# One hand-written order on TensorE, cut down: in latent attention only exact scores and value products stay chained

## The chip, the cores and the metric

The kernel runs on one core of one Trainium2 chip. The metric is the device time of one execution in microseconds (us), as the median of several runs. Engines are named PE (TensorE, the matrix unit), DVE (VectorE), ACT (ScalarE), POOL (GpSimd) and SP (SyncE, which issues the DMAs here).

## What is computed

The reference is a two-layer network over 1024 latent tokens with 256 context tokens in front of them, width 1024, in float32. Each layer modulates its input, projects it, runs three kinds of token mixing side by side (gated linear attention, retention, and softmax attention from a latent), projects back, and ends in a gated convolutional feed-forward part. The change touches only the softmax attention:

```python
def _mla_attend(qn, qr, kn, kr, v):
    s = (jnp.einsum('bqhd,bkhd->bhqk', qn, kn)
         + jnp.einsum('bqhr,bkr->bhqk', qr, kr)).astype(jnp.float32) * MLA_SCALE
    p = jax.nn.softmax(s, axis=-1).astype(v.dtype)
    return jnp.einsum('bhqk,bkhe->bqhe', p, v)
```

There are 8 heads, with 64 plain and 32 rotated features for queries and keys and 64 for values; `qn`, `kn` and `v` are products of two normalised latents (256 and 128 wide). Latent tokens attend to all 1280 tokens, context tokens to the 256 context tokens, and the second layer needs no context output.

## The kernel before

All activations lie with features on partitions and tokens along the free axis. A layer runs in stages: projection of two halves of 640 tokens, then the token mixing, then output projection, layer norm and feed-forward. The token mixing of a layer is one stretch in which two generators are woven together (`weave`, 1.5 steps of `lin` for one of `mla`): `lin` makes the linear attention and retention (lines up to L812, many small operations on every engine), `mla` the softmax attention. Generators fix the order in which instructions are written; the scheduler of the language then places each engine's instructions by priority and by its own estimate of when they are ready. Each engine then executes its own list in order.

`mla` (from L822) makes for each head h:

- production, `prod_kq(h)`: the rotated query rows are copied by DMA (L901), then nine matmuls (seven in the second layer) give plain keys and queries (L912, L915) in PSUM banks 0 to 2; ACT copies them out rounded (L921) and DVE writes the rest that rounding lost (L922). `prod_qr` (L879, L886) makes the rotated queries of four heads, `prod_v` (L867) the values of two.
- `maxima(h)`: rough scores, one matmul each (L934), in three banks taken in turn ("pre", banks 0 to 2), each reduced to a row maximum on DVE (L935): 26 of them in the first layer and 24 in the second. When all are there, one small reduction (L937), a transpose of the maxima on PE (L941), an ACT copy (L942), and two DMAs, out to memory (L943) and back as row 96 of the query tile (L944), so that the exact scores come out with the maximum taken off.
- exact scores, `products` (L951): three matmuls into one of three other banks ("sc", banks 3 to 5), then an exponential on ACT (L1042) into a tile P. Seven such tiles exist.
- `values` (L957): P times V into bank 6. A value or sum product is float32 and shows as two matmuls in the trace. DVE adds P tiles up (L1053), so that only two are left for the sums.
- `quotient`: the sums of P by a product with ones (L969, in a bank of "pre"), reciprocal by ACT and DVE (L974 to L977), product (L981), store (L983).

Head h's scores and values are written together with the production and the maxima of head h+1 (`beside()`, two steps of them for each group of three score matmuls). Two sets of key tiles and two of query tiles exist, so the tiles of head h+2 are those of head h, and their copies (L901) wait for the last score of head h.

What sets the order of these matmuls on PE is `pin`: it adds to each matmul a dependency without a semaphore on the matmul pinned before it, so the scheduler must keep them in the written order:

```python
        def pin(x):
            if prev[0] is not None:
                self.tc.add_manual_dep(x.ins, prev[0].ins.name, ...)
            prev[0] = x
```

Before, every matmul of `mla` is pinned. Those of `lin` are not: they are placed between.

Of the kernel before, what the change touches and what calls it, by code (L numbers as in the profile page):

```python
# [74 lines left out]
class Net:  # L75
# [750 lines left out]
    def mla(self, l, S):  # L826
# [4 lines left out]
        nc, a = self.nc, self.a  # L831
        ww = []
        for k, n in (("uqn", 512), ("uqr", 256), ("ukv", 512)):
            t = self.ws([128, 2, n])
            nc.sync.dma_start(t[:], a[k][l])
            ww.append(t)
        wn, wr, wk = ww
# [8 lines left out]
        def bank(what):  # L846

            turn[what] = (turn[what] + 1) % 3
            return self.ps[:, turn[what] + (3 if what == "sc" else 0), :]

        def three():
            return self.ps[:, base[0]:base[0] + 3, :].rearrange("p a b -> p (a b)")
# [3 lines left out]
        def pin(x):  # L856

            if prev[0] is not None:
                self.tc.add_manual_dep(x.ins, prev[0].ins.name, mybir.DependencyInfo(mybir.DependencyClass.NoSync, mybir.DependencyReason.DATA),
                                       reason="in order")  # L860
            prev[0] = x

        def prod_v(p):
            V[p] = [self.hid([128, 5, 128]) for _ in range(2)]
            ps = three()
            for t_ in range(10):
                pin(nc.tensor.matmul(ps[:, 128 * t_:128 * t_ + 128], S.ckv[:, 128 * t_:128 * t_ + 128], wk[:, 1, 128 * p:128 * p + 128],  # L867
                                 start=True, stop=True))
            for i in range(2):
                nc.scalar.copy(V[p][i][:].rearrange("p a b -> p (a b)"), ps[:, 640 * i:640 * i + 640])  # L870
            yield

        def prod_qr(x):
            QR[x] = [self.yk(F32R), self.yk(F32R)]
            ps, raw = three(), QR[x][1]
            chunks = [(o, min(512, T - o), ps[:, o - lo:min(512 + o, T) - lo]) for o in range(lo, T, 512)]
            for o, n, t in chunks:
                for kc in range(2):
                    pin(nc.tensor.matmul(t, wr[:, kc, 128 * x:128 * x + 128], S.cq[kc][:, o:o + n], start=(kc == 0), stop=(kc == 1)))  # L879
                nc.scalar.copy(raw[:, o:o + n].bitcast(F32), t)  # L880
            for o, n, t in chunks:
                r = raw[:, o:o + n].bitcast(F32)
                t2, co, si = self.tt([128, 512]), self.tt([128, 512]), self.tt([128, 512])
                nc.sync.dma_start(co[:, 0:n], a["mcos"][:, o:o + n])
                nc.sync.dma_start(si[:, 0:n], a["msin"][:, o:o + n])
                pin(nc.tensor.matmul(t, self.permm[:], r, start=True, stop=True))  # L886
                nc.vector.tensor_tensor(t2[:, 0:n], t, si[:, 0:n], op=ALU.mult)
                nc.vector.tensor_tensor(r, r, co[:, 0:n], op=ALU.mult)
                nc.vector.tensor_tensor(r, r, t2[:, 0:n], op=ALU.add)
                self.split(QR[x][0][:, o:o + n], raw[:, o:o + n], r)  # L890
                del t2, co, si
            yield

        def prod_kq(h):
            K = Kt[h % 2]
            Q[h] = [self.hs([128, T]) for _ in range(2)]
            rr = slice(32 * (h % 4), 32 * (h % 4) + 32)
            for x in range(2):
                for o in range(lo, T, 512):
                    c = slice(o, min(o + 512, T))  # L900
                    nc.sync.dma_start(Q[h][x][64:96, c].bitcast(F32), QR[h // 4][x][rr, c].bitcast(F32))  # L901
            if h < 2:
                for b in range(2):
                    cs = slice(640 * b, 640 * b + 640)
                    self.split(K[0][64:96, cs], K[1][64:96, cs], S.kr[b][64:96, :])
            if h == 1:
                S.kr.clear()
            yield
            ps = three()
            for o, t, kb in ((CTX, ps[:, 0:512], 1), (CTX + 512, ps[:, 512:1024], 1), (0, ps[:, 1024:1280], 0)):  # L910
                n = 512 if kb else CTX
                pin(nc.tensor.matmul(t[0:64, 0:n], wk[:, 0, 64 * h:64 * h + 64], S.ckv[:, o:o + n], start=True, stop=True, skip_group_check=True))  # L912
                if o >= lo:
                    for kc in range(2):
                        pin(nc.tensor.matmul(t[64:128, 0:n], wn[:, kc, 64 * h:64 * h + 64], S.cq[kc][:, o:o + n],  # L915
                                         start=(kc == 0), stop=(kc == 1), skip_group_check=True))
            for o, t, n in ((CTX, ps[:, 0:1024], 1024), (0, ps[:, 1024:1280], CTX)):
                for X, r in ((K, 0), (Q[h], 64)):
                    if r and o < lo:
                        continue  # L920
                    nc.scalar.copy(X[0][0:64, o:o + n], t[r:r + 64])  # L921
                    nc.vector.tensor_tensor(X[1][0:64, o:o + n], t[r:r + 64], X[0][0:64, o:o + n].bitcast(F32), op=ALU.subtract)  # L922
            yield

        def maxima(h):

            k0, q0 = Kt[h % 2][0], Q[h][0]
            mx, part = self.sm([128, 10]), self.sm([128, 8, 3])
            for qi in range(lo // 128, 10):
                nk = CTX if qi < 2 else T  # L930
                for j, o in enumerate(range(0, nk, 512)):
                    n = min(512, nk - o)
                    t = bank("pre")[:, 0:n]
                    pin(nc.tensor.matmul(t, q0[0:96, 128 * qi:128 * qi + 128], k0[0:96, o:o + n], start=True, stop=True))  # L934
                    nc.vector.tensor_reduce(mx[:, qi:qi + 1] if qi < 2 else part[:, qi - 2, j:j + 1], t, axis=AX.X, op=ALU.max)  # L935
                    yield
            nc.vector.tensor_reduce(mx[:, 2:10], part[:], axis=AX.X, op=ALU.max)  # L937
            yield
            n = 10 - lo // 128
            t, r = bank("pre"), self.dgt()  # L940
            pin(nc.tensor.matmul(t[0:n, 0:128], mx[:, 10 - n:10], self.ident[:], start=True, stop=True))  # L941
            nc.scalar.activation(r[0:n, :], t[0:n, 0:128], AF.Copy, scale=-1.0)  # L942
            nc.sync.dma_start(S.mx[h, 10 - n:10, :], r[0:n, :].bitcast(F32))  # L943
            nc.sync.dma_start(q0[96:97, lo:T].bitcast(F32), S.mx[h:h + 1].rearrange("h a b -> h (a b)")[:, lo:T])  # L944
            yield
# [14 lines left out]
        def quotient(h, c0, n, sums):  # L960

            r = 64 * (h % 2)
            o, ov, rb, u = ob[h // 2], self.tt([128, n]), self.tt([128, n]), self.tt([128, n])
            nc.scalar.copy(ov[:], self.pb("av")[:, 0:n])
            yield
            t = bank("pre")[:, 0:n]
            for x, P in enumerate(sums):
                for i in range(2):
                    pin(nc.tensor.matmul(t[64 * i:64 * i + 64, :], self.ones[:, 0:64], P[:, i], start=(x == 0), stop=(x == len(sums) - 1),  # L969
                                         skip_group_check=True))  # L970
            sums.clear()
            del P

            nc.scalar.activation(rb[:], t, AF.Ln)  # L974
            nc.scalar.activation(rb[:], rb[:], AF.Exp, scale=-1.0)
            nc.vector.tensor_tensor(u[:], t, rb[:], op=ALU.mult)
            nc.vector.scalar_tensor_tensor(rb[:], u[:], -2.0, rb[:], op0=ALU.add, op1=ALU.mult)  # L977
            yield
            for i in range(2):
                hs = slice(64 * i, 64 * i + 64)  # L980
                nc.vector.scalar_tensor_tensor(o[r:r + 64, c0 + n * i:c0 + n * i + n], ov[hs, :], -1.0, rb[hs, :], op0=ALU.mult, op1=ALU.mult)  # L981
            if h % 2:
                nc.sync.dma_start(S.m[:, 4 + h // 2, c0:c0 + 2 * n], o[:, c0:c0 + 2 * n])  # L983
            yield
# [10 lines left out]
        for _ in chain(prod_v(0), prod_qr(0), prod_kq(0)):  # L995
            yield
# [4 lines left out]
        for h in range(8):  # L1001
# [3 lines left out]
            if h < 7:  # L1005
                if (h + 1) % 4 == 0:
                    g.append(prod_qr((h + 1) // 4))
                g += [prod_kq(h + 1), maxima(h + 1)]
                if (h + 1) % 2 == 0:
                    g.append(prod_v((h + 1) // 2))  # L1010
# [6 lines left out]
            if l == 0:  # L1017
                P = [self.w2([128, 2, 128], F32) for _ in range(2)]
                for kt in range(2):
                    t = bank("sc")[:, 0:256]  # L1020
# [14 lines left out]
            for kt in range(0, 12, 2):  # L1035
                if kt < 10:
                    for k in (kt, kt + 1):
                        held[k] = self.w2([128, 2, 512], F32)
                        for i in range(2):
                            t = bank("sc")  # L1040
# [6 lines left out]
                if kt >= 2:  # L1047
                    for k in (kt - 2, kt - 1):
                        P = held[k]
# [441 lines left out]
```

## Time and profile before

| | us |
|---|---|
| median of three runs (lowest to highest) | 3589.85 (3583.57 to 3593.07) |
| the profiled execution's own time | 3592.44 |
| its span, first to last instruction | 3590.7 |
| PE busy in the span | 3398.0 (95%) |
| DVE busy | 2288.0 (64%) |
| ACT busy | 1433.9 (40%) |
| POOL busy | 329.3 (9%) |
| mean granted clock of PE, share of full | 0.959 |

Busy times are unions of an engine's intervals; matmuls overlap in the record, so a price of one is better read from start to start. "Idle before" counts what an engine waited before a group, with what released it. The granted clock is the share of full speed that PE had. The rows that are used below come from the page, from its tables of busy time by stretch, from its lists of waits, and from its timelines.

### The profile page before, as it was taken

The page shows a single profiled execution, that of the slowest core. Times are in us where ns is not written, and L with a number is a line of the kernel's source. Part 1 is how long each engine was busy: PE and PEld are TensorE (multiplying, and loading weights), DVE is VectorE, ACT ScalarE, POOL GpSimd, SP SyncE. Part 2 cuts the span into 40 slices and gives each one's busy share as a digit, 9 for nine tenths or more (in the row PEclk, how much of TensorE's full clock was granted, in tenths as well). Part 3 has the DMA queues.
Part 4 walks back from the last instruction along what each step waited for, and adds up shares of the span by engine and source line. Part 5 has one row for each costly group of instructions (what it writes and reads, how often), then busy time and mean ns, then how long its engine had stood idle before and what let it go on. Part 6 is the DMA issues. An engine that isn't in the chain of part 4 may idle for free. (4 is left out here: it accounts for less than half of the span.)

```text
span 3590.7 us, 50954 instructions
## 1 busy us (share of the span) xinstructions
PE 3398.0 (95%) x20366; PEld 2762.3 (77%) x20366; DVE 2288.0 (64%) x3467; ACT 1433.9 (40%) x2403; POOL 329.3 (9%) x487
## 2 busy tenths in 40 slices
PE   8997988889999999999999999788899999999998
PEld 6995544445999999999999897444456788888897
DVE  4336686876785444675557645777676775587555
ACT  3333343434363332353333443334334544345433
POOL 0001122211010000000000000222120000000001
PEclk9998897989999999999999998889899999999999
DMA  8554011123223333422223434011014222223221
GB/s 293 198 176 120 28 35 42 34 83 135 71 71 118 118 118 128 149 101 77 77 73 117 170 124 135 19 30 47 30 54 155 94 94 94 97 92 118 94 95 48
DMA packets 174702, 354.64 MB, mean 99 GB/s; under 512 B 15648, under 2 KB 92912, under 8 KB 174464
## 3 DMA queue, kind: packets, MB, share of 16 engines
q1 hardware_dynamic: 174464, 351.38, 29.4%
q8 instruction: 160, 2.62, 0.3%
q14 instruction: 78, 0.64, 0.1%
HBM read 310.09 MB, written 36.51 MB: 97 GB/s over the span
## 5 line engine op out<-in xcount | busy, mean ns | idle before, releaser
L323 PE MATMUL ps<-h,w 128*128 128x320 f32 (+5 forms) x9600 | 1676.0, 335 | 21.4 <-ACT h L212 12.6
L323 PEld LDWEIGHTS ps<-h,w 128*128 128x128 f32 x9600 | 1535.5, 190 | 158.3 <-ACT h L212 14.8
L213 DVE TENSOR_TENSOR w<-ws,w 128x1024 fp32r<-128x1024 f32 x360 | 440.3, 1223 | 589.2 <-PE ps L323 299.6
L1202 PE MATMUL ps<-hid,w 128*128 128x256 f32 (+4 forms) x3696 | 576.5, 316 | 1.5 <-ACT hid L212 1.5
L1202 PEld LDWEIGHTS ps<-hid,w 128*128 128x128 f32 x3696 | 538.8, 189 | 36.1 <-issue 7.6
L212 ACT CAST w<-ws 128x1024 fp32r<-128x1024 f32 x360 | 379.1, 1054 | 410.6 <-PE ps L1202 291.1
L951 PE MATMUL ps<-h,h 96*128 96x512 f32 (+3 forms) x1008 | 317.3, 436 | 3.8 <-DMA h<-mx 2.3
L1042 ACT ACTIVATE w<-ps 128x512 f32<-128x512 f32 x320 | 189.9, 596 | 284.6 <-PE ps L951 280.9
L951 PEld LDWEIGHTS ps<-h,h 96*128 96x128 f32 (+1 forms) x1008 | 189.5, 205 | 107.9 <-issue 70.2
L1169 DVE SCALAR_TENSOR_TENSOR t<-u,vec,t 128x642 f32<-128x642 f32 (+3 forms) x176 | 144.6, 822 | 183.2 <-ACT t L1168 183.1
L935 DVE TENSOR_REDUCE sm<-ps 128x1 f32<-128x512 f32 (+1 forms) x400 | 222.9, 588 | 52.3 <-PE ps L934 50.2
L1163 ACT COPY u<-ps 128x512 f32<-128x512 f32 (+4 forms) x264 | 118.2, 483 | 316.5 <-PE ps L323 316.5
L1207 DVE SCALAR_TENSOR_TENSOR y<-ps,mod,y 128x320 f32<-128x320 f32 (+5 forms) x376 | 197.2, 558 | 67.8 <-PE ps L1202 67.3
L934 PE MATMUL ps<-h,h 96*128 96x512 f32 (+1 forms) x400 | 153.3, 442 | 50.5 <-DVE sm L935 26.5
L1053 DVE TENSOR_TENSOR w<-w,w 128x1024 f32<-128x1024 f32 x128 | 176.8, 1382 | 24.2 <-PE ps L957 18.4
L957 PE MATMUL ps<-w,hid 128*64 128x512 f32 (+1 forms) x704 | 183.7, 618 | 0.0
L716 POOL TENSOR_TENSOR hid<-hid,hid 128x512 f32<-128x512 f32 x108 | 160.6, 1505 | 137.9 <-ACT hid L696 75.3
L1159 POOL MEMSET u<- 128x1 f32 (+1 forms) x264 | 21.2, 102 | 1647.1 <-DVE t L1170 1451.7
L934 PEld LDWEIGHTS ps<-h,h 96*128 96x128 f32 x400 | 84.2, 217 | 99.9 <-DVE sm L935 48.9
L1168 ACT ACTIVATE t<-u,vec 128x642 f32<-128x642 f32 (+3 forms) x176 | 153.7, 873 | 0.4
L1170 DVE SCALAR_TENSOR_TENSOR t<-u,vec,t 128x642 f32<-128x642 f32 (+3 forms) x176 | 144.4, 820 | 11.4
L212 ACT CAST hid<-t 128x642 fp32r<-128x642 f32 (+3 forms) x88 | 59.5, 676 | 204.7 <-DVE t L1174 204.7
(197 smaller groups left out, 2972.4 us busy)
## 6 DMA issues: line engine op xcount, KB each, us to landing
ws<-in_up_dram SPq DMA_DIRECT2D x176, 512.0 KB
ws<-in_down_dram SPq DMA_DIRECT2D x88, 512.0 KB
ws<-in_ada_dram SPq DMA_DIRECT2D x80, 512.0 KB
ws<-in_w_in_dram SPq DMA_DIRECT2D x48, 512.0 KB
ws<-in_w_out_dram SPq DMA_DIRECT2D x32, 512.0 KB
y<-in_ada_dram SPq DMA_DIRECT2D x16, 512.0 KB
ws<-in_w_v_dram SPq DMA_DIRECT2D x16, 512.0 KB
hid<-in_xT_dram SPq DMA_DIRECT2D x16, 320.0 KB
```

What stands on the lines that cost most here:

```text
L212: self.nc.scalar.copy(hi, src)
L213: self.nc.vector.tensor_tensor(lo, src, hi.bitcast(F32), op=ALU.subtract)
L323: nc.tensor.matmul(ps[:, i, 0:n], w_[:, k, :], h[k][:, part, o:o + n], start=(k == 0 and q == 0), stop=(k == 7 and q == 2))
L716: nc.gpsimd.tensor_tensor(X[n][:], blk(E[n][:, 0, cs[i]]), qx[:], op=ALU.mult)
L934: pin(nc.tensor.matmul(t, q0[0:96, 128 * qi:128 * qi + 128], k0[0:96, o:o + n], start=True, stop=True))
L935: nc.vector.tensor_reduce(mx[:, qi:qi + 1] if qi < 2 else part[:, qi - 2, j:j + 1], t, axis=AX.X, op=ALU.max)
L951: pin(nc.tensor.matmul(t, Kt[h % 2][ka][0:rows, 128 * kt:128 * kt + 128], Q[h][qa][0:rows, c0:c0 + n], start=(x == 0), stop=(x == 2)))
L957: pin(nc.tensor.matmul(op[64 * i:64 * i + 64, 0:n], V[h // 2][kt // 5][:, kt % 5, r:r + 64], P[:, i], start=(kt == 0), stop=last, skip_gro ...
L1042: nc.scalar.activation(held[k][:, i], t, AF.Exp, scale=MSCALE)
L1053: nc.vector.tensor_tensor(A[:], A[:], P[:], op=ALU.add)
L1202: nc.tensor.matmul(pb[i][:, 0:n], w[w_][:, x, ms], p.hh[f0 + x][hp][:, o - 1:o - 1 + n], start=(x == 0 and q == 0), stop=(x == gn - 1 and ...
L1207: nc.vector.scalar_tensor_tensor(t, pb[i][:, o:o + n], self.md(l, 5, m, who), t, op0=ALU.mult, op1=ALU.add)
```

## The change

The pin is taken off six kinds of matmul: the value production (L867), the rotated queries (L879, L886), the key and query production (L912, L915), the rough scores (L934), the transpose of the maxima (L941) and the sums' products (L969). The exact scores (L951) and the value products (L957) stay pinned, now only behind each other. No instruction is added or removed: PE executes the same matmuls in another order, within the two token-mixing stretches alone, and the lists of DVE, ACT and SP are ordered anew there too. POOL's list is the same.

```diff
-                pin(nc.tensor.matmul(ps[:, 128 * t_:128 * t_ + 128], S.ckv[:, 128 * t_:128 * t_ + 128], wk[:, 1, 128 * p:128 * p + 128],
-                                 start=True, stop=True))
+                nc.tensor.matmul(ps[:, 128 * t_:128 * t_ + 128], S.ckv[:, 128 * t_:128 * t_ + 128], wk[:, 1, 128 * p:128 * p + 128],
+                                 start=True, stop=True)
...
-                    pin(nc.tensor.matmul(t, q0[0:96, 128 * qi:128 * qi + 128], k0[0:96, o:o + n], start=True, stop=True))
+                    nc.tensor.matmul(t, q0[0:96, 128 * qi:128 * qi + 128], k0[0:96, o:o + n], start=True, stop=True)
```

(and the same at L879, L886, L912, L915, L941 and L969).

Place 1 is PE's list at the production for head 6 in the first layer: the last matmul of production (L915), the matmuls of `lin` (L727), the sums of head 4 (L969), head 5's value products for the context (L957), its exact scores for the latent tokens (L951, from `h_4997` and `h_4998`, head 5's queries), and the first rough scores of head 6 (L934). Before:

```order
L915 MATMUL ps<-y_373,ws_2543 64x256
L727 MATMUL ps<-hid_5366,hid_5335 32x256 x4
L727 MATMUL ps<-hid_5378,hid_5342 32x128 x4
L727 MATMUL ps<-hid_5433,hid_5353 32x128 x4
L969 MATMUL ps<-w_5055,ones 64x512 x2
L969 MATMUL ps<-w_5234,ones 64x512 x2
L957 MATMUL ps<-w_5390,hid_4893 64x128 x2
L957 MATMUL ps<-w_5391,hid_4893 64x128 x2
L951 MATMUL ps<-h_4997,h_2551 128x512
L951 MATMUL ps<-h_4998,h_2551 128x512
L951 MATMUL ps<-h_4997,h_2552 128x512
L934 MATMUL ps<-h_2549,h_5400 128x256 x2
```

After:

```order
L915 MATMUL ps<-y_373,ws_2543 64x256
L951 MATMUL ps<-h_4997,h_2551 128x256
...
L957 MATMUL ps<-w_5390,hid_4893 64x128 x2
L957 MATMUL ps<-w_5391,hid_4893 64x128 x2
L951 MATMUL ps<-h_4997,h_2551 128x512
L951 MATMUL ps<-h_4998,h_2551 128x512
L951 MATMUL ps<-h_4997,h_2552 128x512
...
L727 MATMUL ps<-hid_5366,hid_5335 32x256 x4
...
L969 MATMUL ps<-w_5055,ones 64x512 x2
L969 MATMUL ps<-w_5234,ones 64x512 x2
L934 MATMUL ps<-h_2549,h_5400 128x256 x2
```

The exact scores of the context (six) and eight groups of the latent scores, 24 matmuls, now stand between the production and the sums of head 4; before there were only the twelve matmuls of `lin`.

Place 2 is PE's list at the transpose of head 7's maxima (L941) in the first layer. `h_5400` and `h_5401` are the queries of head 6, `h_5832` those of head 7; L934 is head 7's rough scores, L957 head 6's values. Before:

```order
L934 MATMUL ps<-h_2551,h_5832 128x512
L934 MATMUL ps<-h_2551,h_5832 128x256
...
L727 MATMUL ps<-hid_6103,hid_6068 32x128 x4
L941 MATMUL ps<-ident,sm_5892 10x128
L951 MATMUL ps<-h_5400,h_2549 128x512
L951 MATMUL ps<-h_5401,h_2549 128x512
L951 MATMUL ps<-h_5400,h_2550 128x512
...
L957 MATMUL ps<-w_6154,hid_5706 64x512 x2
L957 MATMUL ps<-w_6169,hid_5706 64x512 x2
L951 MATMUL ps<-h_5832,h_2551 128x256
```

After:

```order
L957 MATMUL ps<-w_6169,hid_5706 64x512
L934 MATMUL ps<-h_2551,h_5832 128x512
L957 MATMUL ps<-w_6169,hid_5706 64x512
L934 MATMUL ps<-h_2551,h_5832 128x512
L934 MATMUL ps<-h_2551,h_5832 128x256
L727 MATMUL ps<-hid_6090,hid_6037 32x256 x4
...
L969 MATMUL ps<-w_5887,ones 64x512
L941 MATMUL ps<-ident,sm_5892 10x128
L969 MATMUL ps<-w_5887,ones 64x512
L727 MATMUL ps<-hid_6152,hid_6037 32x256 x4
...
L735 MATMUL ps<-hm,hid_6116 128x4 x2
L951 MATMUL ps<-h_5832,h_2551 128x256
```

The transpose moved from a place with 18 scores and 12 value products of head 6 behind it to one behind the last of them; between it and head 7's first score stand one product of the sums and matmuls of `lin`.

Place 3 is SP's list around the two DMAs of head 6's maxima (L943, L944); the L901 are the copies for head 7's queries. Before:

```order
L797 DMA u_5868<-v_88 128x2x256
L943 DMA mx_92<-dg_5692 10x128
L944 DMA h_5400<-mx_92 1x1280
L655 DMA hid_5781<-gate_86 128x2x256
L901 DMA h_5832<-y_4538 32x512 x2
L901 DMA h_5832<-y_4538 32x256
L901 DMA h_5833<-y_4539 32x512 x2
L901 DMA h_5833<-y_4539 32x256
```

After:

```order
L797 DMA u_5868<-v_88 128x2x256
L901 DMA h_5832<-y_4538 32x512 x2
L901 DMA h_5832<-y_4538 32x256
L901 DMA h_5833<-y_4539 32x512 x2
L943 DMA mx_92<-dg_5692 10x128
L901 DMA h_5833<-y_4539 32x256
L944 DMA h_5400<-mx_92 1x1280
```

Five of head 7's six copies moved ahead of the store of the maxima, and one lies between it and the load.

## Rows read from the trace of the kernel before

**Rows 1.** The page's first line: the span of the profiled execution.

```profile
span 3590.7 us, 50954 instructions
```

**Rows 2.** Busy time by stretch, both attention stretches: stretch, length, engines, PEclk, DMA share, GB/s.

```profile
354.50:867.00 512.50, 452.14 (x2308) 248.30 (x2301) 389.29 (x619) 204.91 (x430) 126.14 (x96) 0.90 0.15 47
2253.50:2717.00 463.50, 408.59 (x1919) 221.19 (x1913) 347.91 (x514) 177.61 (x349) 103.96 (x79) 0.89 0.14 44
```

**Rows 3.** PE's waits, first layer's stretch: waiter, releaser, total us, times, longest us.

```profile
PE ps L969 <- DVE h L922: 16.4, 4, 8.6
PE ps L934 <- DVE sm L935: 11.0, 11, 1.9
PE ps L941 <- DVE sm L937: 9.2, 5, 3.1
...
PE ps L912 <- DVE t L976: 4.7, 1, 4.7
```

**Rows 4.** PE's waits, second layer's stretch.

```profile
PE ps L934 <- DVE h L922: 10.5, 6, 2.9
PE ps L941 <- DVE sm L937: 9.2, 5, 2.9
PE ps L934 <- ACT h L921: 8.1, 3, 4.7
PE ps L934 <- DVE sm L935: 6.7, 5, 4.1
```

**Rows 5.** PE timeline: start us, length us, group, count, [idle before <-releaser].

```profile
689.15 1.08 PE L727 MATMUL ps<-hid,hid 128*32 128x256 f32 x24
698.86 3.68 PE L969 MATMUL ps<-w,ones 128*64 128x512 f32 x8 [8.63 <-DVE h L922]
```

**Rows 6.** VectorE in the same moment, same columns.

```profile
694.17 1.21 DVE L1053 TENSOR_TENSOR w<-w,w 128x1024 f32<-128x1024 f32 x1
695.30 1.54 DVE L922 TENSOR_TENSOR h<-ps,h 64x1024 fp32r<-64x1024 f32 x2
...
697.58 1.57 DVE L922 TENSOR_TENSOR h<-ps,h 64x1024 fp32r<-64x1024 f32 x2
```

**Rows 7.** PE timeline, prices from start to start: values, exact scores, production.

```profile
446.19 1.94 PE L957 MATMUL ps<-w,hid 128*64 128x512 f32 x8
448.06 0.97 PE L951 MATMUL ps<-h,h 97*128 97x512 f32 x3
448.86 0.52 PE L934 MATMUL ps<-h,h 96*128 96x256 f32 x2
...
2370.71 0.64 PE L912 MATMUL ps<-y,ws 128*64 128x512 f32 x1
...
2374.30 0.97 PE L951 MATMUL ps<-h,h 97*128 97x512 f32 x3
```

**Rows 8.** Timeline from a transpose of maxima to the first score behind it.

```profile
353.74 0.39 PE L941 MATMUL ps<-ident,sm 128*10 128x128 f32 x1 [2.18 <-DVE sm L937]
...
354.38 0.27 ACT L942 ACTIVATE dg<-ps 10x128 fp32r<-10x128 f32 x1 [2.00 <-PE ps L941]
...
354.67 0.36 SPq L943 DMA_DIRECT2D mx<-dg  x1
...
356.27 0.23 SPq L944 DMA_DIRECT2D h<-mx  x1
...
357.94 1.65 PE L951 MATMUL ps<-h,h 97*128 97x256 f32 x6 [2.26 <-DMA h<-mx]
```

**Rows 9.** SP timeline: four of the copies of L901.

```profile
680.08 2.48 SPq L901 DMA_DIRECT2D h<-y  x4
```

**Rows 10.** PE timeline after a longer wait and later.

```profile
560.62 1.11 PE L912 MATMUL ps<-y,ws 128*64 128x512 f32 x1 [4.74 <-DVE t L976]
...
572.13 1.48 PE L951 MATMUL ps<-h,h 97*128 97x512 f32 x3
...
599.70 0.86 PE L951 MATMUL ps<-h,h 97*128 97x512 f32 x3
```

More of the change, by code (lines that the diff above doesn't have):

```diff
@@ L878, in prod_qr @@
                 for kc in range(2):
-                    pin(nc.tensor.matmul(t, wr[:, kc, 128 * x:128 * x + 128], S.cq[kc][:, o:o + n], start=(kc == 0), stop=(kc == 1)))
+                    nc.tensor.matmul(t, wr[:, kc, 128 * x:128 * x + 128], S.cq[kc][:, o:o + n], start=(kc == 0), stop=(kc == 1))
                 nc.scalar.copy(raw[:, o:o + n].bitcast(F32), t)
@@ L885, in prod_qr @@
                 nc.sync.dma_start(si[:, 0:n], a["msin"][:, o:o + n])
-                pin(nc.tensor.matmul(t, self.permm[:], r, start=True, stop=True))
+                nc.tensor.matmul(t, self.permm[:], r, start=True, stop=True)
                 nc.vector.tensor_tensor(t2[:, 0:n], t, si[:, 0:n], op=ALU.mult)
@@ L911, in prod_kq @@
                 n = 512 if kb else CTX
-                pin(nc.tensor.matmul(t[0:64, 0:n], wk[:, 0, 64 * h:64 * h + 64], S.ckv[:, o:o + n], start=True, stop=True, skip_group_check=True))
+                nc.tensor.matmul(t[0:64, 0:n], wk[:, 0, 64 * h:64 * h + 64], S.ckv[:, o:o + n], start=True, stop=True, skip_group_check=True)
                 if o >= lo:
                     for kc in range(2):
-                        pin(nc.tensor.matmul(t[64:128, 0:n], wn[:, kc, 64 * h:64 * h + 64], S.cq[kc][:, o:o + n],
-                                         start=(kc == 0), stop=(kc == 1), skip_group_check=True))
+                        nc.tensor.matmul(t[64:128, 0:n], wn[:, kc, 64 * h:64 * h + 64], S.cq[kc][:, o:o + n],
+                                         start=(kc == 0), stop=(kc == 1), skip_group_check=True)
             for o, t, n in ((CTX, ps[:, 0:1024], 1024), (0, ps[:, 1024:1280], CTX)):
@@ L940, in maxima @@
             t, r = bank("pre"), self.dgt()
-            pin(nc.tensor.matmul(t[0:n, 0:128], mx[:, 10 - n:10], self.ident[:], start=True, stop=True))
+            nc.tensor.matmul(t[0:n, 0:128], mx[:, 10 - n:10], self.ident[:], start=True, stop=True)
             nc.scalar.activation(r[0:n, :], t[0:n, 0:128], AF.Copy, scale=-1.0)
@@ L968, in quotient @@
                 for i in range(2):
-                    pin(nc.tensor.matmul(t[64 * i:64 * i + 64, :], self.ones[:, 0:64], P[:, i], start=(x == 0), stop=(x == len(sums) - 1),
-                                         skip_group_check=True))
+                    nc.tensor.matmul(t[64 * i:64 * i + 64, :], self.ones[:, 0:64], P[:, i], start=(x == 0), stop=(x == len(sums) - 1),
+                                         skip_group_check=True)
             sums.clear()
```

## Prediction

> **What bounds the kernel now.** I read the page first, to see where the order of the changed matmuls matters at all. The span is 3590.7 us [rows 1], but the lists differ only in the two token-mixing stretches, so I next took busy time by stretch from the first to the last work of the heads: 512.5 and 463.5 us, 976 in all [rows 2]. The reader is to see three things there. PE is busy 452.1 and 408.6 us, so it stands idle 60.4 + 54.9 = 115.3 us. DVE is busy 389.3 + 347.9 = 737.2 us, 76% of the two stretches, so it is not full, but it is near enough to be late whenever several of its jobs come at once. And the granted clock is 0.90 and 0.89, so PE also works slower than it does in the dense parts.
>
> Then the lists of PE's waits say who is waited for. In the first layer the largest is the sums' product behind DVE's rest of the production, L969 behind L922: 16.4 us in four waits, the longest 8.6 [rows 3]. In the second layer, where the context has no product of its own, the same lateness falls on the first rough scores: 10.5 us behind L922 and 8.1 behind ACT's L921 [rows 4]. The transposes wait 9.2 us in either layer for their last maxima, and rough scores for a free bank 11.0 and 6.7 us [rows 3, 4]. One production waits 4.7 us for a quotient [rows 3]. These are waits of matmuls that were pinned, and everything that was pinned behind them waited too. The timeline shows it best: the last matmul before the gap starts at 689.15 with a length of 1.08 us, and the next, L969, at 698.86, after 8.63 us in which PE does nothing [rows 5]. Meanwhile DVE is not idle: it adds P tiles and works through L922, the last of it ending near 699 [rows 6]. Head 5's scores needed none of this.
>
> **The change, part by part.** No work is added or removed, so each term is a wait.
>
> *A. Waits at the production* (16.4 + 4.7 in the first layer, 10.5 + 8.1 in the second, 39.7 us [rows 3, 4]). Place 1 shows what moved ahead: 24 score matmuls, eight groups at 0.80 us each (448.06 to 448.86 [rows 7]) = 6.4 us, and about 1.5 us more for the context's scores and values, estimated at the same price per column. Together 7.9 us of new cover. Of the four waits in the first layer only the longest, 8.6, exceeds it, by 0.7 us: some 15 of 16.4 recovered. In the second layer 8 to 13 scores instead of 3 stand before the first rough score, about 10 x 0.27 = 2.7 us of new cover; of its nine waits only 4.7 and 2.9 exceed that, so some 16 of 18.6. Of the 4.7 I take half. Sum: 34 us.
>
> *B. Waits of the transposes* (18.4 us [rows 3, 4]). Between the last rough score and the transpose stood 3 to 15 matmuls of the list before, now 7 to 22. I take half: 9 us. It can't be more than 18.4, and none if DVE is late by more.
>
> *C. Rough scores waiting for a bank* (17.7 us [rows 3, 4]). Their 24 to 26 are now spread over 36 to 54 score matmuls of a head rather than 36 to 42, so DVE gets more time between reductions. I take a third: 6 us; the bounds are nothing and all of it.
>
> *D. The rest* of the 115.3 us are waits of matmuls of `lin` and small ones; nothing in the change speaks to them. I cost them at nothing.
>
> *E. New: the path from the transpose to the next head's first score.* It takes 353.74 to 357.94 = 4.2 us where it was not hidden [rows 8]: transpose, ACT copy, two DMAs one after the other. Before, 18 scores and 12 value products covered it almost everywhere (6 x 0.80 and 1.87 / 4 x 12 = 10.4 us [rows 7]). Now every score of the head is already done (place 2), and what is left are values, production of the next head but one, and `lin`. From the list, with 0.47 us for a value product, 3.59 / 7 = 0.51 for a production matmul [rows 7] and 1.08 us for a dozen of L727 [rows 5], the cover at heads 2 to 7 is 1.9 to 8 us in the first layer and 3.3 to 8 in the second. It falls short of 4.2 only at head 7, by 2.3 and 0.9 us. With some delay of ACT's and SP's own lists I take 6 us lost. Lower bound nothing. Upper bound: SP must issue up to six L901 around the pair (place 3), 2.48 / 4 = 0.62 us each [rows 9], so 4.2 + 3.7 = 7.9 us would be needed, and the shortages at the twelve heads add up to 23 us.
>
> The two DMAs take 356.27 - 354.67 = 1.60 and 357.94 - 356.27 = 1.67 us there [rows 8]. Against this change speaks the Trainium skill, DMA: Bandwidth & Descriptors, section "Anatomy of one DMA — SWDGE (gpsimd) path": a DMA costs some 2.0 us however small, most of it the receipt of the write (fitted on another issuing path than SP's). By it the chain would be an estimated 4.9 us, and the gain about 2 us smaller. I use the row.
>
> *F. Given back.* The recovered 34 + 9 + 6 - 6 = 43 us assume that DVE then delivers. Its share would rise from 76% to 737 / 933 = 79%, and in the gap of [rows 5] it was fully at work [rows 6]; PE running ahead will meet it at the next wait. I take half as given back: 22 us less idle. Bounds: none given back, or all.
>
> *G. Clock.* After the 4.74 us wait a group of three scores takes 1.48 us, and 0.86 later [rows 10]: PE was near its lower level of 1.2 GHz and went back to 2.4. The clock of 0.895 over 976 us [rows 2] costs some 102 us beside 115 us of idle time, 0.89 us for each. Only the longer gaps do this, so I take a third: 22 x 0.3 = 7 us. Bounds: nothing and 0.89.
>
> Sum: 22 + 7 = 29 us. The profiled execution took 3592.4 us; it would take 3563. The median shown is 2.6 us below that execution, so I forecast 3561 us for the median.
>
> **The rivals.**
>
> *DVE takes all of it back* (no change). For it: DVE is at work during the largest gap [rows 6], and an in-order list that is late stays late; the scheduler's estimate of DVE, not the chip's, put the rough scores where they are. Against it: 24% of DVE's time is free [rows 2], and part of that free time is DVE waiting for rough scores that stood behind something else. Time: A to C gain what E costs, about 3588.
>
> *The heads now meet in series* (slower). Place: between the last score of a head and the first of the next. Before, the maxima were ready some 10 us early; now the store of the maxima stands in SP's list behind copies that themselves wait for the last score (place 3), and the last rough scores stand among the last values (place 2), so that DVE's lateness adds to the DMA path. It decides if the path takes 7.9 us rather than 4.2. Price: 23 us of shortage, 23 x 0.89 = 20 us of clock, and A to C bring 12 us only: 31 us slower, 3621. For it: the transposes already wait for DVE in ten of fourteen later heads [rows 3, 4]. Against: the copies wait for scores that are done by then, and values and production cover most of the path.
>
> *More than forecast*: nothing given back in F and half the clock cost recovered, 43 x 1.45 = 62 us, 3528 for the median. For it: the two longest waits have work in front of them now. Against: DVE's share.
>
> *The change does nothing to the order*: excluded, since the three places show other lists.
>
> **How the numbers follow.** A measurement of this kernel can tell about 0.3% from no change, 11 us: faster is below 3579, slower above 3600. The forecast (3528 to 3579) gets 0.45, the larger gain 0.12, no change 0.20, series 0.23. Faster 0.57, same 0.20, slower 0.23. The range must reach into both others: from 3522, which leaves out about half of the larger gain, 0.06, to 3612, which leaves out about half of the slower case, 0.12: 0.18 in all. The forecast's own range is 3528 to 3579.
>
> **What would show it.** Right: the waits of L969 and L934 for L922 and L921 fall from 35 us to under 10; PE's idle time in the two stretches falls from 115 to about 93 us; the clock there rises by a hundredth or so; the waits of L951 for the DMA of the maxima, 2.3 us in one wait before [rows 8], grow to 5 to 10. Wrong: if those grow past 20 us, the heads run in series; if L934 and L941 wait longer for L935 and L937 by what L922 no longer costs, DVE took it back; if the idle time falls and the time does not, the cause lies elsewhere.

## Result, and the profile after

| | before | changed |
|---|---|---|
| median, us | 3586.71 (3578.79 to 3593.07) | 3525.65 (3522.95 to 3530.16) |
| profiled execution's span, us | 3590.7 | 3521.4 |
| ratio, 95% interval | | 0.9832 (0.9807 to 0.9857) |

The change makes the kernel 61 us faster, 1.7%. The forecast was 3561 us: the direction was right, the size less than half of what came (29 of 61 us). 3525.65 lies in the range (3522 to 3612), at its lower edge, and just below the forecast's own range (3528 to 3579).

The stretches of [rows 2] in the changed kernel, same columns (PE, its weight loads, DVE, ACT, POOL busy; PEclk; DMA share; GB/s), cut again from the first work of the heads to the last:

```profile
353.00:850.00 497.00, 465.91 (x2312) 245.84 (x2312) 395.42 (x622) 202.23 (x430) 124.29 (x96) 0.94 0.16 50
2240.20:2647.50 407.30, 397.04 (x1924) 205.91 (x1922) 338.28 (x512) 176.66 (x349) 102.24 (x78) 0.99 0.16 51
```

They are 904.3 us long, where they were 976.0. PE's idle time is 31.1 + 10.3 = 41.4 us, where it was 115.3; its busy time is 863.0, where it was 860.7. So the 72 us by which the stretches shrank are the idle time that went. DVE is busy nearly as long as before (733.7 us, where it was 737.2) in less time: its share is 81%, where it was 76%. The granted clock is 0.94 and 0.99, where it was 0.90 and 0.89. Outside the stretches the changed kernel takes 2.4 us more.

PE's waits in the first layer, as in [rows 3]:

```profile
PE ps L934 <- DVE sm L935: 7.7, 7, 2.2
PE ps L735 <- ACT t L730: 4.9, 1, 4.9
PE ps L951 <- ACT w L1042: 3.0, 3, 1.4
...
PE ps L867 <- DVE sm L935: 2.0, 1, 2.0
...
PE ps L969 <- DVE h L922: 1.5, 1, 1.5
```

and in the second, as in [rows 4]:

```profile
PE ps L727 <- DVE hid L703: 4.0, 2, 3.0
PE ps L934 <- ACT h L921: 2.2, 2, 1.6
PE ps L951 <- ACT w L1042: 1.3, 3, 0.6
PE ps L727 <- ACT t L730: 0.8, 1, 0.8
PE ps L934 <- DVE sm L935: 0.6, 1, 0.6
```

The waits at the production (L969 and L934 for L922 and L921) were 35.0 us and are 3.7. The transposes (L941) are in neither list any more. The wait of a first score for the DMA of the maxima, 2.3 us before [rows 8], is gone, not grown.

PE's timeline at the same production as in [rows 5], head 6 of the first layer:

```profile
664.68 2.31 PE L915 MATMUL ps<-y,ws 128*64 128x512 f32 x7
666.92 0.98 PE L951 MATMUL ps<-h,h 97*128 97x256 f32 x6
668.48 0.71 PE L957 MATMUL ps<-w,hid 128*64 128x128 f32 x8 [0.58 <-ACT w L1022]
669.11 4.24 PE L951 MATMUL ps<-h,h 97*128 97x512 f32 x17
673.28 0.86 PE L727 MATMUL ps<-hid,hid 128*32 128x256 f32 x16
674.93 0.42 PE L727 MATMUL ps<-hid,hid 128*32 128x128 f32 x8 [0.79 <-DVE hid L703]
675.28 1.92 PE L951 MATMUL ps<-h,h 96*128 96x512 f32 x7
678.71 1.94 PE L969 MATMUL ps<-w,ones 128*64 128x512 f32 x8 [1.51 <-DVE h L922]
```

Where PE stood for 8.63 us it now does 24 scores, and the sums wait 1.51 us.

The other border, from head 6's transpose to its first score (L951 at 730.95), and SP's list beside it:

```profile
721.28 0.39 PE L941 MATMUL ps<-ident,sm 128*10 128x128 f32 x2
721.60 1.83 PE L867 MATMUL ps<-ws,y 128*128 128x128 f32 x14
...
727.37 1.50 PE L957 MATMUL ps<-w,hid 128*64 128x512 f32 x5
...
730.95 0.74 PE L951 MATMUL ps<-h,h 97*128 97x256 f32 x4
```

```profile
718.42 3.06 SPq L901 DMA_DIRECT2D h<-y  x5
722.00 0.30 SPq L943 DMA_DIRECT2D mx<-dg  x1
722.35 0.51 SPq L901 DMA_DIRECT2D h<-y  x1
723.28 0.24 SPq L944 DMA_DIRECT2D h<-mx  x1
```

Five of the six copies are issued before the transpose, and the sixth between the store and the load of the maxima. Values, production and `lin` fill the 9.7 us from transpose to score without a gap. At head 7 of the same layer, where the prediction counted the least cover, 10.3 us lie between the transpose and the first score (L951 at 795.10). PE stands idle for 1.8 and 4.9 us of them, but for matmuls of `lin`, not for the DMA of the maxima:

```profile
784.76 0.39 PE L941 MATMUL ps<-ident,sm 128*10 128x128 f32 x2
...
788.91 0.45 PE L727 MATMUL ps<-hid,hid 128*32 128x128 f32 x8 [1.77 <-POOL hid L716]
794.23 1.01 PE L735 MATMUL ps<-hm,hid 128*128 128x4 f32 x4 [4.87 <-ACT t L730]
```

### The profile page after: what moved, and what is told of

The parts are those of the page before. It is cut to its first block, busy times and chain, and to the rows that moved or that the text cites. A ratio compares the mean times of both kernels' runs of the same rounds, so it can differ in the third digit from the quotient of the medians.

```text
span 3521.4 us, 50901 instructions
## 1 busy us (share of the span) xinstructions
PE 3404.1 (97%) x20366; PEld 2745.1 (78%) x20366; DVE 2283.2 (65%) x3467; ACT 1430.1 (41%) x2403; POOL 327.5 (9%) x487
## 5 line engine op out<-in xcount | busy, mean ns | idle before, releaser
L951 PE MATMUL ps<-h,h 96*128 96x512 f32 (+3 forms) x1008 | 302.2, 419 | 4.4 <-ACT w L1042 4.3
L1042 ACT ACTIVATE w<-ps 128x512 f32<-128x512 f32 x320 | 187.8, 596 | 240.2 <-PE ps L951 196.9
L951 PEld LDWEIGHTS ps<-h,h 96*128 96x128 f32 (+1 forms) x1008 | 183.8, 195 | 102.9 <-issue 58.5
L935 DVE TENSOR_REDUCE sm<-ps 128x1 f32<-128x512 f32 (+1 forms) x400 | 223.7, 587 | 61.7 <-PE ps L934 59.9
L957 PE MATMUL ps<-w,hid 128*64 128x512 f32 (+1 forms) x704 | 231.3, 596 | 0.7 <-ACT w L1022 0.6
L934 PE MATMUL ps<-h,h 96*128 96x512 f32 (+1 forms) x400 | 155.0, 435 | 20.1 <-DVE sm L935 14.6
L716 POOL TENSOR_TENSOR hid<-hid,hid 128x512 f32<-128x512 f32 x108 | 157.4, 1474 | 165.1 <-ACT hid L696 129.2
L934 PEld LDWEIGHTS ps<-h,h 96*128 96x128 f32 x400 | 77.9, 207 | 101.9 <-DVE sm L935 46.1
```

The lines of the kernel that those rows point to most:

```text
L716: nc.gpsimd.tensor_tensor(X[n][:], blk(E[n][:, 0, cs[i]]), qx[:], op=ALU.mult)
L951: pin(nc.tensor.matmul(t, Kt[h % 2][ka][0:rows, 128 * kt:128 * kt + 128], Q[h][qa][0:rows, c0:c0 + n], start=(x == 0), stop=(x == 2)))
L957: pin(nc.tensor.matmul(op[64 * i:64 * i + 64, 0:n], V[h // 2][kt // 5][:, kt % 5, r:r + 64], P[:, i], start=(kt == 0), stop=last, skip_gro ...
L1042: nc.scalar.activation(held[k][:, i], t, AF.Exp, scale=MSCALE)
```

## The experiments

Ratios are to the kernel before, measured beside each on the same chip, with 95% intervals.

**One kind of matmul freed at a time, from the kernel before.** The pin is taken off only the production; only the sums; only the rough scores and transposes. The edits are lines of the change's own diff; for the production:

```diff
-                pin(nc.tensor.matmul(t[0:64, 0:n], wk[:, 0, 64 * h:64 * h + 64], S.ckv[:, o:o + n], start=True, stop=True, skip_group_check=True))
+                nc.tensor.matmul(t[0:64, 0:n], wk[:, 0, 64 * h:64 * h + 64], S.ckv[:, o:o + n], start=True, stop=True, skip_group_check=True)
```

(and L867, L879, L886, L915).

> From the kernel before, only the production matmuls (values, rotated queries, keys and queries) lose their pin; rough scores, transposes and sums stay chained with scores and values. Theory 'each wait goes with the pin of the matmul that waits': nearly nothing, 0 to -8 us, because the matmuls that waited (sums, rough scores, transposes) keep their pin. Rival 'one decoupling': also small, 0 to -15 us, because whatever stays pinned still ties the scores to VectorE. More than -30 us would say that the place of the production alone was the cause.

> From the kernel before, only the sums' products lose their pin. Theory 'each wait goes with its own pin': the 16.4 us that they waited in the first layer behind the production's rest go, and some clock with them, -15 to -25 us. Rival 'one decoupling': the first rough score behind them takes over the wait, 0 to -10 us; then waits of the rough scores behind L922 and L921 appear in the first layer as they stand in the second.

> From the kernel before, only the rough scores and the transposes of their maxima lose their pin. Theory 'each wait goes with its own pin': the 36 us of their waits for reductions and the 19 us behind the production in the second layer go, the sums' 16 us stay: -35 to -50 us. Rival 'one decoupling': the sums keep the scores tied in both layers, under -25 us.

Measured: production 0.9939 (0.9919 to 0.9959), some 22 us of 3590; sums 0.9987 (0.9968 to 1.0006), not told from nothing; rough scores and transposes 0.9937 (0.9919 to 0.9955), some 23 us. The first is more than either theory gave; the second speaks for the rival, though in another way than it said, and the third lies at its edge, half of what the own-pin theory asked. With the sums alone freed, PE's waits in the first layer read:

```profile
PE ps L934 <- DVE sm L935: 13.1, 13, 2.4
PE ps L969 <- DVE h L922: 11.4, 3, 7.3
PE ps L941 <- DVE sm L937: 11.2, 5, 3.7
PE ps L912 <- DVE t L976: 4.7, 1, 4.7
```

The sums still wait 11.4 us (why the scheduler left them there is not shown), and the rough scores wait 2 us more for banks than in [rows 3], the transposes 2 us more for their maxima; waits of rough scores for L922 or L921, which the rival named, are not there. The three parts together give 0.6 + 0.1 + 0.6 = 1.4%.

**Two chains instead of one.** Scores and values in one, everything else in another, both in the written order:

```diff
-        prev = [None]
+        prev, prev2 = [None], [None]
...
-        def pin(x):
+        def pin2(x):
+            pin(x, prev2)
+
+        def pin(x, prev=prev):
```

(with `pin2` at L867, L879, L886, L912, L915, L934, L941, L969).

> From the kernel before, two chains in place of one: scores and values in one, all other matmuls of the attention in the other, each in its written order. If the gain is the decoupling of the two, all of it comes: -50 to -65 us. If the free placement of each production matmul and rough score by the scheduler matters, clearly less than the change: -20 to -40 us.

Measured: 0.9805 (0.9777 to 0.9832), median 3522.43. All of the gain comes with nothing placed freely within either chain. What paid is that scores and values no longer stand in one line with the work that waits for DVE. DVE, ACT and SP have another order here too, as they have by the change; no run keeps theirs as it was, so what that adds is not told apart.

**No pins at all**, twice, the second time beside the changed kernel itself on one chip. The edit takes `pin` off L951 and L957 too.

> No matmul pinned at all. If what the pins did was only to tie the scores to VectorE's work, this is as fast as the change, within 10 us of 3526. If the order between scores and value products is worth a pin, it is slower than the change by more than that: values are placed late, P tiles stay held and scores wait for the exponentials.

> The changed kernel once more, beside no pins at all and beside the two with VectorE relieved, on one chip. Expected as measured before: a ratio of 0.983 to the kernel before.

> No pins at all, once more beside the changed kernel. If the pins that are left cost something, its ratio lies at least 0.003 below that of the changed kernel; if they only do nothing, the intervals overlap and the medians lie within 10 us.

Measured: 0.9792 (0.9766 to 0.9819) the first time; then 0.9790 (0.9768 to 0.9813), median 3519.39, against 0.9806 (0.9782 to 0.9830), median 3524.78, for the changed kernel. The intervals overlap and the medians lie 5 us apart: the pins that the change leaves can't be told from none.

**More work for DVE, in both kernels.** Of a head's reductions nine (eight in the second layer) are done twice:

```diff
                     nc.vector.tensor_reduce(mx[:, qi:qi + 1] if qi < 2 else part[:, qi - 2, j:j + 1], t, axis=AX.X, op=ALU.max)
+                    if qi % 2 == 0 and j < 2:
+                        nc.vector.tensor_reduce(mx[:, qi:qi + 1] if qi < 2 else part[:, qi - 2, j:j + 1], t, axis=AX.X, op=ALU.max)
```

> The kernel before with nine (first layer) or eight (second) of a head's reductions done twice on VectorE, 136 more reductions in all, some 78 us of VectorE at 0.59 us each, most of them 512 wide. Theory 'one in-order chain hands VectorE's lateness on': a good part of it shows, +30 to +70 us. Rival 'VectorE is not what PE waits for': under +15 us.

> The changed kernel with the same 136 reductions done twice. If VectorE takes back what PE gains, as the prediction assumed with its half given back, it is full in the stretches and nearly all 78 us show on top of the changed kernel: at or above 3590 us. If it has room there, since its share was 81%, a minor part shows: +10 to +40 us on the changed kernel, about 3535 to 3565 us.

Measured: before, 1.0171 (1.0147 to 1.0196), some 61 us more; changed, 0.9985 (0.9972 to 0.9998), median 3588.3, 55 to 64 us above the changed kernel by its two ratios, 0.9832 and 0.9806 (below). My expectation of room in the changed kernel was wrong. The time that I gave for a full DVE was nearly right, though DVE is not full there (82% of the heads' stretches): most of the added work shows in either kernel. The heads' stretches with it, cut a little later, at the first matmul of the next stage; first the kernel before, then the changed one:

```profile
361.57:901.70 540.13, 457.81 (x2309) 250.21 (x2302) 423.97 (x687) 207.33 (x433) 126.59 (x97) 0.88 0.15 48
2287.73:2778.82 491.09, 423.11 (x1922) 225.37 (x1914) 378.82 (x571) 179.23 (x349) 102.76 (x78) 0.87 0.14 42
...
358.44:883.40 524.96, 476.89 (x2312) 251.06 (x2311) 425.60 (x689) 203.45 (x433) 123.03 (x96) 0.90 0.16 49
2271.06:2713.61 442.55, 413.71 (x1920) 212.49 (x1916) 365.93 (x569) 177.34 (x348) 104.15 (x78) 0.95 0.15 47
```

Cut alike, the stretches were 983.0 and 907.6 us without it. So the heads take 48.3 us more for 60.2 us more of DVE in the kernel before, and 59.9 us more for 56.0 in the changed one, in one execution each. Most of what is left of the cost, 10.4 and 5.1 us, lies ahead of the heads, where head 0's reductions are made.

PE's idle time in the changed kernel with it is 48.1 + 28.8 = 76.9 us, against 44.9 without it, cut alike, and in the first layer the longest total is that of scores waiting for exponentials, which had 3.0 us (L953 is L951, L1044 is L1042, and L937 is the added reduction here):

```profile
PE ps L953 <- ACT w L1044: 9.7, 7, 3.2
PE ps L934 <- DVE sm L935: 8.6, 10, 3.0
PE ps L934 <- DVE sm L937: 8.0, 5, 2.7
```

The added reduction also keeps its bank of rough scores longer. Over both layers L934 waits 24.4 us for L935 and L937 here, where it waited 8.3 us, and 39.7 us in the kernel before with the added work, where it waited 17.7. How much of the cost is this and how much DVE's longer list, no run takes apart.

**Less work for DVE.** Two of a head's eight additions of P tiles go to GpSimd:

```diff
-                            nc.vector.tensor_tensor(A[:], A[:], P[:], op=ALU.add)
+                            (nc.gpsimd if k % 5 == 1 else nc.vector).tensor_tensor(A[:], A[:], P[:], op=ALU.add)
```

> The changed kernel with two of a head's eight additions of P tiles moved from VectorE to GpSimd, 32 in all, 1.36 us each: 43 us less for VectorE. If VectorE's list sets the pace of the heads in the changed kernel too, as the added reductions suggest (some 55 us for 78), the time falls by 15 to 40 us. If PE, busy 95% of the heads' stretches, is the bound now, it stays within 10 us; and if the additions, slow on GpSimd, are late themselves, P tiles stay held and it gets slower by 10 us or more.

> The kernel before with the same 32 additions moved to GpSimd. If what the one chain cost was VectorE's lateness at the heads' borders, where the additions stand in front of the production's rest, this recovers part of it with the chain left as it was: -15 to -40 us. If they come late from GpSimd, slower by 10 us or more.

Measured: changed 0.9896 (0.9869 to 0.9923), 32 us slower than the changed kernel beside it; before 1.0139 (1.0112 to 1.0165), 50 us slower. DVE was hardly relieved. Its busy time in the heads is 731.1 us in the changed kernel with this edit, where it was 735.5 cut alike, and 754.1 in the kernel before with it, where it was 742.6. In the changed kernel DVE's own additions take 30 us less in all, but other lines of it take more (L693 46.5 us where it took 38.6, L750 27.4 where it took 21.3). And the additions come late: one takes 2.40 us on GpSimd in the median, against 1.22 on DVE (the line's instructions in the changed kernel with this edit):

```profile
L1053 DVE TENSOR_TENSOR w<-w,w x96: 1207/1224/3137, 392.4 to 2675.0; 128x1024 f32<-128x1024 f32 x96
...
L1053 POOL TENSOR_TENSOR w<-w,w x32: 2339/2404/3162, 390.0 to 2668.4; 128x1024 f32<-128x1024 f32 x32
...
who waited for it (us, times):
  DVE w L1053: 24.3, 10
```

DVE's next addition waits for it in its in-order list. GpSimd's work for `lin` comes later too: in the first layer L727 waits 9.1 us for L716, where it waited 1.8. So these runs don't tell whether a lighter DVE would help. The edit costs the one-chain kernel more, 50 us against 32, but with intervals of some 10 and 13 us that difference is only just clear of noise.

**A longer path for the maxima, in the changed kernel.** One more DMA, from memory to memory:

```diff
             nc.sync.dma_start(S.mx[h, 10 - n:10, :], r[0:n, :].bitcast(F32))
+            nc.sync.dma_start(S.mx2[h, 10 - n:10, :], S.mx[h, 10 - n:10, :])
-            nc.sync.dma_start(q0[96:97, lo:T].bitcast(F32), S.mx[h:h + 1].rearrange("h a b -> h (a b)")[:, lo:T])
+            nc.sync.dma_start(q0[96:97, lo:T].bitcast(F32), S.mx2[h:h + 1].rearrange("h a b -> h (a b)")[:, lo:T])
```

> The changed kernel with one more DMA in the path of the maxima, from memory to memory, some 1.6 us or more at each of 16 heads. If the path from the transpose to the next head's first score is on the path that sets the end (the prediction's term E, and its rival 'in series'), it costs 16 times that, +20 us and more on the changed kernel. If other work covers it, under +8 us, and the first scores' wait for the DMA of the maxima stays under 5 us.

Measured: 0.9844 (0.9820 to 0.9869), 4 and 14 us above the changed kernel's two ratios. The first is what I expected of a covered path, the second lies between the two expectations. The intervals overlap, and no score waits for the DMA of the maxima in its trace. At head 6 the added DMA (L944 here, the load is L945) delays the load by 2.04 us, from 719.47 to 721.51:

```profile
719.47 0.50 SPq L944 DMA_DIRECT2D mxx<-mx  x1
721.51 0.24 SPq L945 DMA_DIRECT2D h<-mxx  x1
```

Sixteen times 2.04 us would be 33 us. More than half of it, if not all, lies under other work.

## Where the prediction was right, and where it failed

*What bounds the kernel* was right: PE's idle time in the heads' stretches, made by scores that queue behind matmuls that wait for DVE. The two chains show that the tie between the two is what cost the time: without it all of the gain comes, with the written order kept in either chain.

*A*, 34 of 39.7 us: right. The waits for L922, L921 and L976 at the production fell from 39.7 to 3.7 us, so 36 came. *B*, 9 of 18.4: too small; all of it came. *C*, 6 of 17.7: 9.4 came, since 8.3 are left.

*D*, nothing: wrong. Beside A to C the list of before holds 39.5 us; after, 41.4 - 3.7 - 8.3 = 29.4 are left. Some 11 of these are waits of the attention's own matmuls, where some 9 were before. So it is the matmuls of `lin` that wait less, by some 12 us; why, no run takes apart.

*E*, 6 us lost: wrong. No first score waits for that DMA any more, and the added DMA costs less than half of its 33 us. I had counted the cover between transpose and score too low: it is 9.7 us at head 6, and at head 7, where I had counted 1.9, 10.3 us pass. The rival "in series" fell with this. The cited section of the Trainium skill, DMA: Bandwidth & Descriptors, "Anatomy of one DMA — SWDGE (gpsimd) path", would have taken 2 us more off the gain; with the path covered neither its 2.0 us nor the 1.6 us of [rows 8] shows as a wait of a score.

*F*, half given back: this is the step that failed most, the term worth 22 us. Idle time fell by 73.9 us, where the sum had 22. Of the 52 us between them F is 22, and D 10, B 9, E 6, C 3 and A 2 are the rest. What was recovered was not given back: the one new wait of the attention's matmuls for DVE is 2.0 us (L867 behind L935). I had read DVE's 76% and its full hands during the largest gap as a limit that would take PE's lead back. But the waits before were not the price of DVE's total work; they were the time in which one late result stopped matmuls that didn't need it. The doubled reductions show that DVE's work does count, but in both kernels: 48.3 us for 60.2 before, 59.9 us for 56.0 in the changed one. DVE's lateness now has another way to PE: in the changed kernel exponentials wait 33.7 us for additions that still read a P tile, where none did before, but scores wait only 4.3 us for exponentials.

*G*, 7 us from the clock: not shown, and its reading of [rows 10] was wrong. The slow scores at 572.13 don't stand in the low clock around the 4.74 us wait. The granted clock was 0.50 from 558 to 564, 0.98 from 564 to 570, and 0.50 again from 576 to 594; before this second fall PE had waited 2.73 and 1.56 us. So it was not only the longer gap that the lower level of 1.2 GHz followed. Over the stretches the granted clock rose from 0.895 to 0.963, but PE's busy time stayed (860.7 and 863.0), and the idle time alone accounts for the 72 us. A busy time with modelled ends and overlap can't say what the clock gave.

The rival "DVE takes all of it back" had the right thing in sight, DVE's weight, and the wrong conclusion. "More than forecast", which put the median at 3528, was the nearest, and I gave it 0.12. Its time is near by luck: it added 43 us of idle time and 19 us of clock, where 73.9 us of idle time went.

What stays open: why freeing the production alone gives 22 us, more than either theory (in its trace PE stands idle 15 us less in the heads and is busy 10 us less), which part of D came from where, and what the new order of DVE, ACT and SP adds.

## What to carry over

In an in-order queue, look for instructions that wait on another engine and ask who stands behind them without needing the result. One chain over both kinds makes every wait common; two chains, or none, give the independent work its cover back, and freeing one kind while another still ties the two gives only part. Here a helper engine at 76% was no reason to discount the gain: a discount belongs on waits that are named and that have no other work in front of them.

## What the runs showed that I had not expected

A quarter of DVE's time is free in the heads of the kernel before, and yet 60.2 us more work for it there (802.8 against 742.6, cut at the next stage) made the heads 48.3 us longer. Both engines being partly idle at once does not mean that either has room. And work moved off DVE need not make it lighter: 32 additions of 1.36 us each went to GpSimd in the changed kernel, and DVE's busy time in the heads fell by 4 us.
